# An order of instructions from a list scheduler in the source, in place of the framework's own, for a four-layer hybrid model

## The chip, the cores and the metric

One Trainium2 chip, one core of it. The time is the device time of one execution in microseconds, as a median of several runs; one further execution was taken with the hardware profiler, and all rows of traces come from that one. The core has five engines that each work off their own queue in order: TensorE (PE: matmuls, with PEld for its weight loads), VectorE (DVE), ScalarE (ACT), GpSimd (POOL) and SyncE (SP, which here only issues transfers). They wait for one another by semaphores.

## The reference

A model of two blocks on 256 tokens of width 1024 in float32. Each block has two layers, and each layer is a feed-forward network, a mixer and another feed-forward network, each behind an RMS norm and added to the residual stream. A final norm follows each block.

```python
def swiglu(h, w_gate, w_up, w_down):          # width 1024 -> 2816 -> 1024
    return (jax.nn.silu(h @ w_gate) * (h @ w_up)) @ w_down

def hybrid_layer(x, ...):                     # block 1
    x = x + 0.5 * swiglu(rmsnorm(x, ffn1_norm), ffn1_wg, ffn1_wu, ffn1_wd)
    proj = rmsnorm(x, mix_norm) @ w_in
    na_o = rmsnorm(merge_heads(neighbourhood_attention(...)), na_gain)
    o_fwd = gla_chunked(qg, kg, vg, log_gf, True)
    o_bwd = flip(gla_chunked(flip(qg), flip(kg), flip(vg), flip(log_gb), False))
    gla_o = merge_heads(rmsnorm(o_fwd + o_bwd, gla_gain)) * jax.nn.silu(g_r)
    x = x + jnp.concatenate([na_o, gla_o], axis=-1) @ w_out
    x = x + 0.5 * swiglu(rmsnorm(x, ffn2_norm), ffn2_wg, ffn2_wu, ffn2_wd)
```

Block 2 has the same frame. Its mixer joins a causal forgetting attention, a dilated causal attention with a partial rotary embedding of its queries and keys (the "rope"), and a gated linear recurrence (HGRN2), whose output is multiplied by a sigmoid gate.

## The kernel before

*Activations.* They are kept with features on partitions and the 256 tokens along the free dimension. Every float32 product is made of three products of a faster type: a weight tile `raw` of 128 x 1024 is loaded, ScalarE writes its high part `whi` (L163) and VectorE the remainder `wlo` (L164); the activations are held as `xhl`, high and low side by side. A block of 128 x 128 weights then takes one matmul of 512 columns (high weights by high and low activations) and one of 256 (low weights by high activations). `blocks` issues these two blocks at a time, so four matmuls. `total` (L270, L271) adds the two halves of a finished bank.

*Stages.* There are 12 stages and two final norms, one after another. A feed-forward stage has 44 groups of 8 blocks (gate and up columns in turn; bank tag `acc`, 3 buffers), each followed by ScalarE, VectorE and GpSimd work (`gate`, `up`), and then 176 blocks for the way down (`o`). A mixer stage has 16 such groups and some chunks of projections that come out by rows (`wi`), the attention work and an output projection of 64 blocks (`o`).

*Mixer1* (block 1) runs a gated linear attention in `gla`: `psC`, `psZ` and `log_sigmoid` make the gates (Abs, then Exp and Ln, L650 and L626), `cumulate` scans them into `C` (L660), GpSimd forms differences of `C` for eight levels (`kq`, L928 to L939), ScalarE takes Exp, VectorE multiplies by keys and queries (L946), and TensorE makes the scores `psA`. The first of the `psA` need keys and queries that `columns` writes (L564). Beside it `na` runs the neighbourhood attention: `psS`, a softmax, `psP`, and values whose slabs are moved by transfers on the SP queue (`slabs`). Its keys come from `columns`, too (L560).

*Mixer2* (block 2) runs `hgrn` with the same level scheme (`X`, differences on GpSimd at L1155 to L1160, products at L1168 and L1169), and `attention`, which begins with the rope (VectorE, L1195 to L1197) and the transposes `psT` (L228, from `heads_T`).

*Norms.* `Stage.norm` sums squares on TensorE (`psN`), takes a root on GpSimd (L281) and spreads it over partitions on TensorE (`psR`). The matmuls of a stage don't need it; their results are multiplied by it later (`rb`). `feed_parts` writes the next stage's `xhl` (L328, L329), `feed_squares` its squares, whose sum is built on GpSimd (L342).

*What sets the order.* A driver (`Driver.run`) runs through jobs (weight tiles in order) and tasks (generators), and records instructions in the order in which a clock of its own, which counts TensorE's time alone, lets them go on; the table `WAIT` holds estimated latencies. The framework then schedules each engine, with the recorded order as priority and with a timing model of its own. By hand there is more: `later` puts GpSimd's transfers behind the last product of a feed-forward gate, `issue_after` puts set-up work behind a split, and `exp_ln` and `gate` place the loads of ScalarE's function tables (at L622 and L1065). A split is recorded one job ahead (`AHEAD`); `raw`, `whi` and `wlo` have four buffers each.

## Time and profile before

| | us |
|---|---|
| median of three runs | 2082.66 |
| lowest and highest run | 2081.74, 2084.51 |
| the profiled execution | 2085.31 |
| its span, first to last instruction | 2083.2 |
| TensorE busy in the span | 2032.4 |
| VectorE busy | 1546.6 |
| ScalarE busy | 1159.0 |
| GpSimd busy | 504.1 |

In the rows, L217 is the line of every matmul and L228 that of every transpose, so TensorE's work is told apart by tile names. Ends of matmuls are modelled and weight loads (PEld) run beside them. The granted TensorE clock stands at one of two levels, 1.2 or 2.4 GHz; a mean of 0.95 in a stretch says that a tenth of it was granted the lower one. The stages of the profiled execution begin at about 0, 197.9 (Mixer1), 338, 523.7, 702.6 (Mixer1), 843, 1027.6, 1217.5 (Mixer2), 1368.4, 1553.3, 1738.1 (Mixer2) and 1889.5 us.

### The profile page before, as it was taken

Reading aid. Unit: us, or ns where it says so; the run is one execution under the profiler, and the core shown is the slowest. Engines: PE = TensorE matmul, PEld = TensorE weight load, DVE = VectorE, ACT = ScalarE, POOL = GpSimd, SP = SyncE. Lnnn points to the kernel's source line nnn. Section 1 sums busy time; section 2 is a strip of 40 time slices with the busy share of each in tenths; the row PEclk is TensorE's granted clock in tenths of the full one; section 3 lists DMA queues with packets and bytes.
Section 4 is the critical chain, followed back from the end, with each engine's and each line's share of the span. In section 5 each row is a group of like instructions: output and inputs, shape, how many; then the busy total and the mean of one; then the engine's idle time right before and its main releaser. Section 6 shows DMA issues by size and latency. Waiting matters only on the chain.

```text
span 2083.2 us, 34135 instructions
## 1 busy us (share of the span) xinstructions
PE 2032.4 (98%) x12620; PEld 1781.7 (86%) x12620; DVE 1546.6 (74%) x2433; ACT 1159.0 (56%) x2038; POOL 504.1 (24%) x502
## 2 busy tenths in 40 slices
PE   8999899999999999999999998999999999899997
PEld 7888788888888888888888897888888889788886
DVE  7776878786776687876687679687767766968764
ACT  6554556554555556555465464565546546456553
POOL 3451503441221141222232103022112210302210
PEclk9999899999999989999999999999999999999998
DMA  7665445655555544555565553455555555345552
GB/s 230 193 194 179 127 126 187 196 186 191 187 188 191 158 130 132 192 191 186 170 205 187 189 161 99 126 185 190 191 183 192 186 188 161 93 132 183 192 190 94
DMA packets 104631, 357.37 MB, mean 172 GB/s; under 512 B 13460, under 2 KB 15012, under 8 KB 104464
## 3 DMA queue, kind: packets, MB, share of 16 engines
q1 hardware_dynamic: 101040, 352.20, 52.8%
q0 software_dynamic: 3136, 2.47, 0.6%
q8 instruction: 99, 1.62, 0.3%
q14 instruction: 68, 0.56, 0.1%
q10 hardware_dynamic: 288, 0.52, 0.1%
HBM read 351.98 MB, written 1.51 MB: 170 GB/s over the span
## 4 chain that ended last, share of the span: by engine, by line
PE 87%; DVE 6%; ACT 2%; POOL 2%; issue 1%; DMA 0%; SPq 0%; DVEq 0%; ACTq 0%; POOLq 0%
PE acc L217 53%; PE o L217 26%; PE wi L217 3%; DVE wlo L164 2%; PE psS L217 2%; PE psA L217 1%; PE psO L217 1%; DVE xhl L329 1%; ACT whi L163 1%; DVE x L438 1%; POOL kq L938 1%; DVE rope L1195 1%; PE psN L217 0%; PE psP L228 0%; POOL kq L936 0%
## 5 line engine op out<-in xcount | busy, mean ns | idle before, releaser
L163 ACT ACTIVATE whi<-raw 128x1024 fp32r<-128x1024 f32 (+3 forms) x682 | 706.7, 1038 | 710.8 <-PE acc L217 388.9
L217 PE MATMUL acc<-xhl,whi 128*128 128x512 f32 x3328 | 1061.6, 400 | 6.1 <-DVE xhl L329 5.9
L164 DVE TENSOR_TENSOR wlo<-raw,whi 128x1024 fp32r<-128x1024 f32 (+3 forms) x682 | 824.0, 1209 | 321.8 <-ACT whi L163 319.3
L217 PEld LDWEIGHTS acc<-xhl,wlo 128*128 128x128 f32 x3328 | 629.4, 189 | 147.3
L217 PE MATMUL acc<-xhl,wlo 128*128 128x256 f32 x3328 | 660.9, 279 | 0.0
L217 PEld LDWEIGHTS acc<-xhl,whi 128*128 128x128 f32 x3328 | 513.1, 190 | 13.0 <-DVE xhl L329 7.2
L217 PE MATMUL o<-hT,whi 128*128 128x512 f32 x1408 | 442.4, 395 | 0.3 <-DVE hT L259 0.3
L465 POOL TENSOR_TENSOR s<-s,rb 128x256 f32<-128x256 f32 x176 | 242.4, 1377 | 666.2 <-ACT s L464 661.8
L217 PEld LDWEIGHTS o<-hT,wlo 128*128 128x128 f32 x1408 | 264.5, 188 | 62.5
L217 PE MATMUL o<-hT,wlo 128*128 128x256 f32 x1408 | 276.6, 278 | 0.0
L217 PEld LDWEIGHTS o<-hT,whi 128*128 128x128 f32 x1408 | 214.4, 189 | 0.7 <-DVE hT L259 0.7
L342 POOL TENSOR_TENSOR sqs<-sqs,sq 128x256 f32<-128x256 f32 x88 | 79.0, 901 | 485.6 <-ACT sq L340 485.2
L271 DVE TENSOR_TENSOR t<-acc,b 128x256 f32<-128x256 f32 x416 | 172.6, 416 | 9.0 <-ACT b L270 9.0
L270 ACT ACTIVATE b<-acc 128x256 f32<-128x256 f32 x416 | 151.7, 367 | 12.4 <-PE acc L217 12.3
L217 PE MATMUL wi<-whi,xhl 128*128 128x352 f32 (+2 forms) x448 | 122.5, 344 | 0.0
L475 DVE TENSOR_TENSOR t<-t,s 128x256 f32<-128x256 f32 x176 | 75.9, 431 | 46.3 <-POOL s L465 44.9
L438 DVE SCALAR_TENSOR_TENSOR x<-o,x 128x256 f32<-128x256 f32 x192 | 77.8, 419 | 37.6 <-PE o L217 35.8
L217 PEld LDWEIGHTS wi<-whi,xhl 128*128 128x128 f32 x448 | 83.5, 195 | 0.8 <-ACT proj L536 0.2
L217 PE MATMUL o<-xhl,whi 128*128 128x512 f32 x256 | 80.9, 397 | 1.4 <-DVE xhl L259 1.4
L464 ACT ACTIVATE s<-t 128x256 f32<-128x256 f32 x176 | 70.5, 400 | 19.7 <-DVE t L463 19.6
L463 DVE TENSOR_TENSOR t<-t,rb 128x256 f32<-128x256 f32 x176 | 75.3, 428 | 5.3
L259 DVE TENSOR_TENSOR hT<-t,hT 128x256 fp32r<-128x256 f32 x176 | 78.4, 445 | 0.9 <-ACT hT L258 0.9
(234 smaller groups left out, 1453.3 us busy)
## 6 DMA issues: line engine op xcount, KB each, us to landing
raw<-in_gu_dram SPq DMA_DIRECT2D x350, 512.0 KB, 3.4
raw<-in_wd_dram SPq DMA_DIRECT2D x176, 512.0 KB, 3.4
raw<-in_win_dram SPq DMA_DIRECT2D x64, 512.0 KB, 3.6
raw<-in_wo_dram SPq DMA_DIRECT2D x32, 512.0 KB, 3.6
raw<-in_win_dram SPq DMA_DIRECT2D x24, 384.0 KB, 3.1
raw<-in_win_dram SPq DMA_DIRECT2D x24, 352.0 KB, 3.3
raw<-in_win_dram SPq DMA_DIRECT2D x8, 388.0 KB, 3.1
proj<-proj SPq DMA_DIRECT2D x32, 64.0 KB, 2.0
```

The source lines that it names most:

```text
L163: self.mark = nc.scalar.activation(hi[:, s], r[:, s], AF.Copy).ins
L164: self.mark_v = nc.vector.tensor_tensor(lo[:, s], r[:, s], hi[:, s].bitcast(F32), op=OP.subtract).ins
L217: c.nc.tensor.matmul(out, l, r, start=start, stop=stop)
L259: c.nc.vector.tensor_tensor(lo, src, hi.bitcast(F32), op=OP.subtract)
L270: c.nc.scalar.activation(b, ps[:, T:], AF.Copy)
L271: c.nc.vector.tensor_tensor(t, ps[:, :T], b, op=OP.add)
L342: adder.tensor_tensor(self.sq[:, j], self.sq[:, j], d, op=OP.add)
L438: nc.vector.scalar_tensor_tensor(xs, acc[g][:, h * T:(h + 1) * T], scale, xs, op0=OP.mult, op1=OP.add)
L463: nc.vector.tensor_tensor(t, t, self.rb, op=OP.mult)
L464: nc.scalar.activation(s, t, AF.Silu)
L465: c.pool_mark = nc.gpsimd.tensor_tensor(s, s, self.rb, op=OP.mult).ins
L475: nc.vector.tensor_tensor(t, t, self.s, op=OP.mult)
```

## The change

All engine calls go to a `Program`, which records them instead of issuing them. A recorded instruction is an `Op` with its engine, an occupancy, a latency, and the earlier ones that it depends on, found from the regions of the tiles that it reads and writes. Matmuls recorded without another instruction between them form one `Op`; `cut` ends it, after each two blocks among other places. `order` then goes through simulated time: of all engines' instructions whose dependencies are met and whose tiles have a buffer, it takes the one that can start first, and among those of equal start the one recorded first. Tiles of one tag are opened in recorded order. `issue` sends the instructions out in that order under `manual_schedule`, so that the framework keeps it and adds only the waits.

The durations are formulas. `set_table` records the load of a function table whenever an activation's function needs another table than the last; the load waits for the users of the old table, and the users of the new one for it. The driver's order of recording, the tiles, the buffer counts and the arithmetic stay. `later`, `issue_after` and `exp_ln` go.

```diff
+class Program:
+    HOP = 0.06
+    DRAIN = 0.17
+    TABLES = {"E": "natural_log_exp_and_others", "S": "silu_and_others"}
+    FUNCS = {AF.Exp: "E", AF.Ln: "E", AF.Silu: "S", AF.Sin: "S"}
...
+    def cost(self, engine, name, args, kw, out, n):
+        if name == "dma_start":
+            return (1.0 if engine == "gpsimd" else 0.43), 2.0
+        if engine == "scalar":
+            return 0.08 + 0.000865 * n + (0.1 if "accum_out" in kw else 0.0), 0.095
+        if engine == "vector":
+            if name == "tensor_tensor_scan":
+                return 0.32, 0.085
+            return 0.07 + 0.001045 * n, 0.085
+        if engine == "gpsimd":
+            if kw.get("op") is OP.pow:
+                return 0.75 if n < 3 else 1.0, 0.05
+            return (0.15 if n < 64 else 0.3) if name == "memset" else 0.4 + 0.0039 * min(n, 260), 0.05
+        return 0.0, 0.0
...
+    def set_table(self, t):
+        if t == self.table:
+            return
+        self.cut()
+        op = Op(len(self.ops), "scalar")
+        self.ops.append(op)
+        op.calls.append(("preload_act_table_set", (self.TABLES[t],), {}))
+        op.occ, op.lat = 1.28, 0.0
+        for u in self.users:
+            op.deps[u] = False
+        self.table, self.load, self.users = t, op, []
...
+                if r.dtype == F32R:
+                    occ = max(m / 2400.0 + (0.02 if m > 256 else 0.0085), 0.109)
+                else:
+                    occ = 2 * max(m / 1200.0, cols / 1200.0, 0.025) / (2 if mode == (64, 64) else 1) + 0.005
+            if op.mode is not None and op.mode != mode:
+                occ += 0.09
...
+    def order(self):
...
+            for e in stale:
+                best[e] = None
+                for op in avail[e]:
+                    at = opening(op)
+                    if at is None:
+                        continue
+                    est = max(op.ready, at, free[e])
+                    k = (est, op.n)
+                    if best[e] is None or k < best[e][0]:
+                        best[e] = (k, op)
+            stale = set()
+            e = min((x for x in engines if best[x]), key=lambda x: best[x][0])
+            (start, _), op = best[e]
...
+            extra = 0.1 if e == "tensor" and mode not in (None, op.mode) and op.mode else 0.0
...
+            free[e] = start + op.occ + extra
+            end = free[e] + op.lat
+            if op.calls[0][0] == "dma_start":
+                dst = op.calls[0][1][0]
+                size = free_size(dst) * dst.shape[0] * 4
+                dma = max(dma, start + 0.5) + size / 300e3
+                end = dma + 1.3
...
+    def issue(self):
+        for op in self.order():
+            e = getattr(self.nc, op.engine)
...
         while self.next < N or self.tasks:
+            self.c.nc.cut()
             if self.run_task():
...
         for ps, hi, lo, x, first, last in two:
             mm(c, ps[:, :T], lo, x[:, :T], False, last)
+        c.nc.cut()
...
-    def exp_ln(self, after):
-        if self.table is None:
-            with self.c.tc.issue_after(after.ins):
-                self.table = self.c.nc.scalar.preload_act_table_set("natural_log_exp_and_others").ins
...
-    nc = c.nc = tc.nc
+    nc = c.nc = Program(tc.nc)
...
     dr.run()
+    with tc.manual_schedule():
+        nc.issue()
```

## Rows read from the trace of the kernel before

**Rows 1.** The page, busy us (share of the span) and instructions by engine.
```profile
PE 2032.4 (98%) x12620; PEld 1781.7 (86%) x12620; DVE 1546.6 (74%) x2433; ACT 1159.0 (56%) x2038; POOL 504.1 (24%) x502
```

**Rows 2.** Table by stage: stretch, width, busy us by engine, clock, DMA share, GB/s.
```profile
0.00:22.30 22.30, 16.25 (x65) 13.04 (x66) 12.95 (x21) 14.13 (x28) 6.09 (x16) 0.85 0.68 217
...
197.90:338.00 140.10, 132.81 (x1058) 118.57 (x1057) 108.55 (x176) 82.27 (x153) 40.70 (x45) 0.95 0.46 141
...
523.70:702.60 178.90, 178.90 (x1030) 156.17 (x1031) 130.82 (x198) 98.04 (x168) 36.35 (x29) 1.00 0.58 185
...
1027.60:1217.50 189.90, 187.98 (x1076) 164.13 (x1077) 139.84 (x225) 103.54 (x177) 44.09 (x39) 0.99 0.58 187
...
1738.10:1889.50 151.40, 143.97 (x1019) 127.35 (x1020) 120.04 (x210) 88.10 (x174) 26.08 (x25) 0.97 0.41 126
```

**Rows 3.** Chain that ended last, in order of time: start, us, what.
```profile
527.03 114.26 PE acc L217 x656
641.29 61.31 PE o L217 x352
```

**Rows 4.** Waits, whole span: waiter <- waited for, total us, times, longest.
```profile
ACT whi L163 <- PE acc L217: 388.9, 335, 3.4
...
PE psT L228 <- DVE proj L1197: 14.3, 3, 6.8
...
PE psS L217 <- DVE proj L560: 5.9, 2, 3.1
PE acc L217 <- DVE xhl L329: 5.9, 6, 2.8
...
PE psA L217 <- DVE proj L564: 5.4, 2, 2.7
...
PE psR L217 <- POOL rstd L358: 1.9, 1, 1.9
```

**Rows 5.** Table by stretch, columns as in rows 2: Mixer1, then Mixer2 (last).
```profile
208.00:220.00 12.00, 12.00 (x68) 10.15 (x67) 7.85 (x16) 8.02 (x14) 1.81 (x3) 1.00 0.46 144
220.00:231.00 11.00, 8.27 (x62) 7.58 (x61) 7.61 (x11) 3.79 (x5) 11.00 (x15) 0.71 0.30 97
231.00:252.00 21.00, 17.93 (x181) 15.91 (x180) 20.59 (x25) 13.40 (x21) 17.71 (x15) 0.91 0.52 142
...
1778.00:1788.00 10.00, 3.22 (x18) 2.82 (x17) 10.00 (x9) 5.11 (x11) 9.62 (x9) 0.83 0.12 39
```

**Rows 6.** Tile `rope`, whole span: duration ns least/median/most, first and last start.
```profile
L1195 DVE TENSOR_TENSOR rope<-proj,cs x16: 211/1084/1153, 1255.7 to 1781.4; 128x64 f32<-128x64 f32 x16
```

**Rows 7.** GpSimd by line at 1770 to 1788: busy us, mean ns | idle before.
```profile
L1159 POOL TENSOR_TENSOR X<-C 128x512 f32<-128x512 f32 x5 | 5.3, 1063 | 36.6 <-DVE C L660 36.6
```

**Rows 8.** VectorE in order of time, Mixer2: start, us, what.
```profile
1776.66 0.76 DVE L1195 TENSOR_TENSOR rope<-proj,cs 128x64 f32<-128x64 f32 x5
...
1779.36 3.14 DVE L1195 TENSOR_TENSOR rope<-proj,cs 128x64 f32<-128x64 f32 x3
...
1785.52 1.10 DVE L1197 TENSOR_TENSOR proj<-rope 128x64 f32<-128x64 f32 x1
```

**Rows 9.** VectorE and TensorE in order of time, Mixer1, 222 to 226.
```profile
224.80 0.86 DVE L564 SCALAR_TENSOR_TENSOR proj<-t,rb 128x256 f32<-128x256 f32 x1
...
225.72 0.65 PE L217 MATMUL psA<-proj 64*64 64x64 f32 x7 [2.73 <-DVE proj L564]
```

**Rows 10.** Groups by line and form, GpSimd's slowest level term.
```profile
L938 POOL TENSOR_TENSOR kq<-C 128x256 f32<-128x256 f32 x14 | 17.1, 1219 | 0.0
```

**Rows 11.** Groups by line and form: splits, `xhl`, table loads.
```profile
L163 ACT ACTIVATE whi<-raw 128x1024 fp32r<-128x1024 f32 x622 | 658.6, 1060 | 667.3 <-PE acc L217 372.0 <-PE o L217 197.1 <-issue 73.0
...
L329 DVE SCALAR_TENSOR_TENSOR xhl<-x,gains,xhl 128x256 fp32r<-128x256 f32 x88 | 70.6, 809 | 6.8 <-ACT xhl L328 6.8
...
L622 ACT ACT_TABLE_LOAD x4 | 5.1, 1283 | 0.1
```

More of the change, by code (lines that the diff above doesn't have):

```diff
@@ L94, with __init__, _then, __getitem__ @@
     [(g, f) for g in range(EARLY, 8) for f in range(8)]
+class View:
+    __slots__ = ("tile", "shadow", "chain", "made")
+    def __init__(self, tile, shadow, chain=()):
+        self.tile, self.shadow, self.chain, self.made = tile, shadow, chain, None
+    def _then(self, name, *args, **kw):
+        return View(self.tile, getattr(self.shadow, name)(*args, **kw), self.chain + ((name, args, kw),))
+    def __getitem__(self, k):
+        return self._then("__getitem__", k)
+    def rearrange(self, *args, **kw):
+        return self._then("rearrange", *args, **kw)
+    def unsqueeze(self, i):
+        return self._then("unsqueeze", i)
+    def to_broadcast(self, shape):
+        return self._then("to_broadcast", list(shape))
+    def bitcast(self, dt):
+        return self._then("bitcast", dt)
+    def pattern(self, offset, ap):
+        return View(self.tile, self.tile.shadow, self.chain + (("pattern", (offset, ap), {}),))
+    @property
+    def shape(self):
+        return self.shadow.shape
+    @property
+    def dtype(self):
+        return self.shadow.dtype
+    def real(self):
+        if self.made is None:
+            r = self.tile.real()
+            for name, args, kw in self.chain:
+                if name == "pattern":
+                    r = bass.AP(tensor=r.tensor, offset=r.offset + args[0], ap=args[1])
+                else:
+                    r = getattr(r, name)(*args, **kw)
+            self.made = r
+        return self.made
+    def region(self):
+        t = self.tile
+        ap, off = self.shadow.ap, self.shadow.offset
+        p0, f0 = divmod(off, t.row)
+        if any(c[0] == "pattern" for c in self.chain):
+            return 0, 1 << 30, 0, 1 << 30
+        n = ap[0][1] if ap[0][0] == t.row else 1
+        if t.bank:
+            return p0 // 32 * 32, -(-(p0 + n) // 32) * 32, 0, 1 << 30
+        rest = ap[1:] if ap[0][0] == t.row else ap
+        return p0, p0 + n, f0, f0 + 1 + sum((c - 1) * st for st, c in rest)
@@ new lines, with __init__, real @@
+class LazyTile:
+    def __init__(self, pool, shape, dtype, kw, shadow):
+        self.pool, self.shape, self.dtype, self.kw, self.shadow = pool, shape, dtype, kw, shadow
+        self.row = 1
+        for n in shape[1:]:
+            self.row *= n
+        self.bank = pool.bank
+        self.tag = (pool.name, kw["tag"])
+        self.bufs = kw.get("bufs") or pool.bufs
+        self.marks, self.left, self.made, self.opened, self.index, self.end = [], 0, None, False, None, 0.0
+    def real(self):
+        if self.made is None:
+            self.made = self.pool.pool.tile(list(self.shape), self.dtype, **self.kw)
+        return self.made
@@ new lines, with __init__, tile @@
+class Pool:
+    def __init__(self, program, pool, name, bufs, bank=False):
+        self.program, self.pool, self.name, self.bufs, self.bank = program, pool, name, bufs, bank
+    def tile(self, shape, dtype, **kw):
+        t = LazyTile(self, shape, dtype, kw, self.program.shadow(tuple(shape), dtype))
+        return View(t, t.shadow)
+class Op:
+    __slots__ = ("n", "engine", "calls", "occ", "lat", "deps", "after", "wait", "ready", "start", "tiles", "mode")
+    def __init__(self, n, engine):
+        self.n, self.engine, self.calls, self.occ, self.lat = n, engine, [], 0.0, 0.0
+        self.deps, self.after, self.wait, self.ready, self.start = {}, [], 0, 0.0, None
+        self.tiles, self.mode = {}, None
@@ L864, in prepare @@
         self.wg = c.cp.tile([33, 512], F32, tag="wgate", name="wgate")
-        with c.later():
-            nc.gpsimd.dma_start(self.wg, a["wgate"][l])
+        nc.gpsimd.dma_start(self.wg, a["wgate"][l])
         rp = a["rpb"]
@@ L1097, in hgrn @@
             e = t2(c, "lse")
-            last = nc.scalar.activation(e, z, AF.Abs)
+            nc.scalar.activation(e, z, AF.Abs)
             gs.append(z)
@@ L1290, in setup1 @@
     yield 20.0
-    with c.later():
-        c.mk = c.cp.tile([P, 7, 64], I32, tag="mk", name="mk1")
-        nc.gpsimd.dma_start(c.mk, a["mk1"])
-        c.nam = c.cp.tile([P, 4, 32], F32, tag="nam", name="nam")
-        nc.gpsimd.dma_start(c.nam, a["nam"])
+    c.mk = c.cp.tile([P, 7, 64], I32, tag="mk", name="mk1")
+    nc.gpsimd.dma_start(c.mk, a["mk1"])
+    c.nam = c.cp.tile([P, 4, 32], F32, tag="nam", name="nam")
+    nc.gpsimd.dma_start(c.nam, a["nam"])
     c.dr.fire("set1")
```

308 lines of the change are left out of this document (225 added, 83 removed).

## The prediction

> **What bounds the kernel now.** I read the page's busy times first, then the busy table by stage, then the chain of waits, then the list of what TensorE waited for. TensorE is busy 98% of the span and VectorE 74% [rows 1], so the kernel is TensorE's, and an order of instructions can only give back what TensorE does not use. The table by stage says where that is [rows 2]. In a feed-forward stage there is nothing: 178.90 us wide, 178.90 busy, clock 1.00. The chain agrees: 656 matmuls, all `acc`, stand in one piece of 114.26 us without a wait, 352 of `o` in 61.31 [rows 3], which is 348.3 ns for each pair of a 512-wide and a 256-wide matmul in both. That pitch is the floor of the eight feed-forward stages: (704 + 352) / 2 pairs x 0.3483 = 183.9 us each, 1,471 of 2083 us, and no order changes it.
>
> What is lost is in the rest [rows 2]. A Mixer1 layer has 140.10 - 132.81 = 7.3 us of idle TensorE and a mean clock of 0.95: a tenth of the layer, 14 us, at 1.2 GHz instead of 2.4, which costs at most 7.0 us. Together 14.3, and there are two such layers: 28.6. A Mixer2 layer has 7.4 us idle and a clock of 0.97: 9.1 us at 1.2 GHz, at most 4.5 us; together 11.9, two layers: 23.8. The stage after the first block's final norm loses 1.9 us idle and, at 0.99, up to 1.9 by the clock: 3.8. In the list of TensorE's waits [rows 4] stage starts wait for `xhl` 5.9 us, of which I put the longest (2.8) down to the kernel's start, where the input still lands; 3.1 are left. Sum of what an order could give: 28.6 + 23.8 + 3.8 + 3.1 = 59 us, so no order ends below about 2024. The start (22.30 us wide, 16.25 busy [rows 2]) and the tail are chains of a landing input and of a last normalisation; I leave both as they are, within 1 us.
>
> **What holds TensorE up there.** All large waits name VectorE: `psT` for the rope 14.3 us, `psS` for L560 5.9, `psA` for L564 5.4 [rows 4]. TensorE goes in the order of the recorded program, so it stands at an attention matmul while weights for later groups wait. But in the same stretches VectorE is full: 20.59 of 21.00 us at 231 to 252, and 10.00 of 10.00 us at 1778 to 1788, where TensorE does 3.22 [rows 5]. And it is full of slow work. A rope product of 64 elements takes 211 ns at best and 1084 in the median [rows 6], because GpSimd's subtractions of 1.06 us stand back to back beside it [rows 7]: three products take 3.14 us [rows 8]. The same holds, weaker, for L564 in Mixer1: 0.86 us for one product of 256 columns, where the wait of 2.73 us ended [rows 9].
>
> This is where the Trainium skill speaks against the change: the page "SBUF — State Buffer", section "SBUF: two separate sides", says that a VectorE instruction with two SBUF inputs and a GpSimd instruction exclude each other for a whole instruction, whichever starts first. The trace agrees (211 against 1084 ns). A scheduler that gives each engine its own duration can't see such a lock; by that rule the waits for the rope would stay, and that part of the sum is zero.
>
> **The change part by part.** *TensorE's order.* Its work is cut into units of four matmuls (two pairs, 2 x 0.348 = 0.7 us), and the scheduler starts the first unit that is ready by its own clock, the earliest recorded first. In Mixer1 the groups behind the waiting `psA` and `psS` need only `xhl` and split weights, so filler exists: at 220 to 231 ScalarE is busy 3.79 of 11 us and at 208 to 220 VectorE 7.85 of 12 [rows 5], and splits can be moved there up to the four buffers. In addition the gate chain that starts the level work (`psC`, `psZ`, Abs, Exp, Ln, `C`) no longer waits behind whole groups of 2.8 us. And the level terms on GpSimd are charged at 0.4 + 0.0039 x 256 = 1.40 us by the code, where the trace has 1.22 or less [rows 10]: they are late in the plan and early on the chip, so TensorE isn't led to them too soon. Against it: VectorE full for 21 us cannot be ordered away, and a filler used early is missing at the end of the layer, where the output projection waits for the attention. The two bounds are 0 and 14.3 us per layer. I take half, 7 us, since of the 7.3 idle the first wait (2.73) has an idle VectorE and ScalarE ahead of it and the second (3.1 of the 5.9 [rows 4]) has not. Two layers: 14 us.
>
> In Mixer2 the plan charges a rope product 0.07 + 0.001045 x 64 = 0.14 us. Eight of them and four sums of the same size are 12 x 0.14 = 1.7 us in the plan, and took 10 us on the chip (1776.66 to 1786.6) [rows 8]. So `psT` is put where TensorE reaches it at the same time as now or earlier, and the wait stays. Bounds: the whole 11.9 us per layer, if the rope gets in front of the subtractions, and minus 3 us, if TensorE gets there at about 1777 and not, as now, at 1786.6 - 6.8 = 1779.8 [rows 4, 8]. I take 2 us per layer, for the small waits around it: 4 us.
>
> *Norms and stage starts.* After the final norm TensorE stands at `psR` for a root on GpSimd, 1.9 us [rows 4], while further groups need no root for their matmuls; the sums are taken out of the banks without it. The scheduler can go past it: 3.5 of 3.8 us. At the other stage starts, a third group can be begun while `xhl` is late; but `xhl` on VectorE takes 0.81 us in the mean [rows 11], and the plan has 0.42 for it. I take 2.5 of 3.1.
>
> *Table loads.* They become instructions that wait only for the last user of the old table, so the load of 1.28 us ahead of the first Exp [rows 11] goes into ScalarE's idle time instead of between Abs and Exp. It is on the gate chain and inside the 7 and 2 us above, not added.
>
> *Splits and loads.* In the feed-forward stages ScalarE already waits 388.9 us for a buffer that TensorE frees [rows 4]: splits can't go earlier, and the weight loads on SP, which wait for the raw tiles that the splits free, neither. Zero, hidden by those buffers; if the plan put a split just ahead of a chain step, one split of 1.06 us [rows 11] would be its price, and VectorE's idle quarter covers it. The slab transfers of Mixer1 go in the same SP queue, and one that the plan puts behind a raw load that has no tile yet would hold them up; I take nothing for it. GpSimd's small transfers lose their fixed place behind a feed-forward product; GpSimd waits most of such a stage, so nothing either.
>
> *Finer interleaving.* Changing between narrow and full matmuls is charged 0.09 to 0.1 us in the plan. The trace has no row for it alone; a mixer that changed 20 times more would pay 2 us, and none if units of one kind stay together, as they do when they come ready together. I take zero and keep 4 layers x 2 = 8 us for the range.
>
> Sum: 14 + 4 + 3.5 + 2.5 = 24 us. The profiled execution took 2085.31 us (span 2083.2); it would take about 2061, and the median of the runs, 2082.66, becomes 2058.5.
>
> **The rivals.** *A. Nearly all is filled.* The plan starts Mixer1's chain so early that its VectorE work spreads out, and the rope gets ahead of the subtractions: 45 to 59 of the 59 us come back, 2024 to 2038. For it: the idle VectorE at 208 to 220. Against it: the full VectorE later on.
>
> *B. The waits move.* The order is another, but VectorE's full stretches decide in both mixers, and what is filled early is waited for before the output projection: only the norms and stage starts gain, 4 to 8 us, or nothing: 2075 to 2083. That the order comes out nearly as now, because with ties the recorded order decides, gives the same time.
>
> *C. Slower: the plan's clock is wrong and the order is fixed.* A unit that stands where the plan has it ready waits for all that the chip is late. The 24 rope instructions of the two layers are about 24 x 0.87 = 21 us later than at their best [rows 6], and 14.3 of it is waited for now [rows 4]; if `psT` is put at the planned end, the rest comes on top: 7 us. At 11 stage starts `xhl` is 0.4 us later than planned: 4 us more, if the units behind it are put up to it. Together with the 8 us of changes, if nothing is gained in Mixer1: 2083 + 7 + 4, up to 8 = 2094 to 2102. It decides as soon as the lateness that newly hits TensorE exceeds the idle time filled, some 5 us per mixer.
>
> **How the numbers follow.** The forecast, a partial gain of 13 to 38 us (2045 to 2070), 0.45. A, with what lies between it and the forecast (2024 to 2045): 0.17. B with the rest of the middle (2070 to 2087): 0.17. C: 0.21. The range 2030 to 2094 leaves out the end of A and most of C. A measurement of this kernel tells a change from none at about 0.2%, 4.2 us: faster means below 2078.5 (0.45 + 0.17 + half of B, 0.08 = 0.70), the same 0.09, slower 0.21.
>
> **What would show it.** Right: the 656-matmul pieces stay at 114.26 us; in the table by stage Mixer1 gets near 133 us and Mixer2 stays near 149; the `psT` wait for L1197 is still the largest of TensorE's waits; the `psR` wait is gone. Wrong: `psT` no longer waits (A), a new wait for `xhl` L259 ahead of the output projection of 5 us or more (B), or idle TensorE inside the feed-forward stages, which I hold to be impossible to gain and easy to lose (C).

## The result and the profile after

The kernel after takes 2061.46 us in the median of four runs (2060.64 to 2062.75), the kernel before, on the same chip, 2083.24. The ratio is 0.9896, with a 95% interval from 0.9879 to 0.9913. The forecast was 2058.5, with a range from 2030 to 2094. The profiled execution of after took 2062.75 us with a span of 2061.0, 22.2 less than before's span of 2083.2.

In the trace of after every instruction has the line of the helper that issues it (L448, in other kernels of this study a line near it), so it is read by tile names. The page's busy times, which answer to [rows 1], and the two pieces of the chain that answer to [rows 3]:

```profile
PE 2023.6 (98%) x12620; PEld 1773.1 (86%) x12620; DVE 1581.3 (77%) x2433; ACT 1198.2 (58%) x2039; POOL 486.8 (24%) x502
```

```profile
337.14 114.27 PE acc L448 x656
451.41 61.31 PE o L448 x352
```

The floor stands: the 656 matmuls take 114.27 us, as before. So the 22 us came from other places, and a table by stage shows which. For it both traces are cut at the last matmul of each `o`, so that a stage's start belongs to it. Columns: stretch, width, then busy us of PE, PEld, DVE, ACT and POOL with their instruction counts, PE's granted clock, DMA share, GB/s. First the kernel before, in this order: the kernel's start with the first feed-forward stage, Mixer1 of the first and second layer, the feed-forward stage after the first block's final norm, Mixer2 of the third and fourth layer.

```profile
0.00:197.90 197.90, 191.85 (x1074) 166.27 (x1075) 144.75 (x216) 110.59 (x192) 73.69 (x94) 0.98 0.63 200
197.90:331.30 133.40, 126.77 (x1023) 113.52 (x1023) 103.56 (x169) 79.14 (x147) 39.15 (x43) 0.95 0.45 137
...
702.60:836.20 133.60, 127.22 (x1023) 113.97 (x1023) 103.60 (x169) 79.16 (x147) 39.19 (x45) 0.95 0.44 136
...
1022.00:1211.50 189.50, 187.58 (x1073) 163.74 (x1073) 139.84 (x225) 103.54 (x178) 44.96 (x40) 0.99 0.58 188
1211.50:1361.60 150.10, 142.57 (x1020) 126.68 (x1019) 119.00 (x220) 87.12 (x170) 26.68 (x29) 0.97 0.41 123
...
1732.20:1882.70 150.50, 143.66 (x1019) 127.33 (x1018) 118.08 (x207) 87.26 (x171) 25.46 (x24) 0.97 0.40 123
```

The same six stages of the kernel after, and between them one plain feed-forward stage (512.70 on):

```profile
0.00:199.00 199.00, 192.99 (x1073) 166.44 (x1074) 150.75 (x228) 116.60 (x194) 73.78 (x104) 1.00 0.64 200
199.00:326.90 127.90, 123.75 (x1024) 110.76 (x1023) 105.97 (x170) 78.74 (x148) 63.66 (x78) 0.97 0.49 147
...
512.70:697.50 184.80, 184.80 (x1066) 161.36 (x1065) 137.62 (x202) 106.54 (x172) 33.67 (x30) 1.00 0.57 185
697.50:819.60 122.10, 120.78 (x1024) 108.49 (x1023) 103.55 (x172) 79.60 (x152) 43.34 (x46) 1.00 0.50 155
...
1005.40:1193.20 187.80, 186.51 (x1074) 162.53 (x1073) 142.60 (x215) 106.36 (x172) 38.15 (x33) 1.00 0.58 185
1193.20:1342.00 148.80, 142.95 (x1019) 127.17 (x1018) 119.67 (x218) 87.00 (x171) 28.36 (x28) 0.97 0.40 125
...
1712.50:1860.40 147.90, 143.24 (x1020) 127.42 (x1019) 118.74 (x208) 88.23 (x172) 26.53 (x23) 0.97 0.42 126
```

By widths: Mixer1 gains 5.5 and 11.5 us, Mixer2 1.3 and 2.6, the stage after the final norm 1.7, and the start loses 1.1. That is 21.5 of the 22.2; the six plain feed-forward stages hold the other 0.7, all of it in the one behind the first Mixer1 layer (186.5 before, 185.8 after). In the second Mixer1 layer TensorE's idle time went from 6.4 to 1.3 us and the clock from 0.95 to 1.00, with the same VectorE work (103.6 us). VectorE's full stretch was not shortened: before, it is busy 26.35 of the 30 us from 722.6 on, where TensorE does 25.40; after, it is busy 39.50 of the 40 us from 717.5 on, and TensorE does 38.68. TensorE only does not stand in front of it any more. Mixer2 still has 4.7 to 5.9 us idle and a clock of 0.97.

What TensorE waited for in after (waiter <- waited for, total us, times, longest), to be read against [rows 4]:

```profile
PE psT L448 <- DVE proj L448: 10.0, 4, 4.9
PE acc L448 <- DVE xhl L448: 2.9, 6, 1.6
PE o L448 <- DVE xhl L448: 2.8, 2, 1.8
...
PE psA L448 <- DVE kq L448: 2.6, 4, 0.7
PE acc L448 <- DVE t L448: 1.6, 2, 1.1
...
PE psR L448 <- POOL rstd L448: 0.8, 2, 0.6
```

The waits of `psS` (5.9) and `psA` (5.4) for `proj` are gone, `psT` for the rope is still the largest. Three questions follow: is it the order of TensorE that gained, why is Mixer1's first layer 5.8 us longer than its second, and what holds Mixer2.

### The profile page after: what moved, and what is told of

Its sections match the earlier page's. It is cut to its first block, busy times and chain, and to the rows that moved or that the text cites. A ratio compares the mean times of both kernels' runs of the same rounds, so it can differ in the third digit from the quotient of the medians.

```text
span 2061.0 us, 33817 instructions
## 1 busy us (share of the span) xinstructions
PE 2023.6 (98%) x12620; PEld 1773.1 (86%) x12620; DVE 1581.3 (77%) x2433; ACT 1198.2 (58%) x2039; POOL 486.8 (24%) x502
## 4 chain that ended last, share of the span: by engine, by line
PE 86%; DVE 9%; ACT 2%; issue 2%; DMA 1%; SPq 0%; POOL 0%; DVEq 0%; ACTq 0%
PE acc L448 51%; PE o L448 26%; PE wi L448 3%; DVE wlo L448 3%; PE psS L448 2%; PE psA L448 1%; DVE x L448 1%; DVE xhl L448 1%; PE psO L448 1%; DVE proj L448 1%; ACT whi L448 1%; DVE t L448 1%; PE psP L448 1%; DVE rope L448 0%; DVE C L448 0%
## 5 line engine op out<-in xcount | busy, mean ns | idle before, releaser
L448 PE MATMUL acc<-xhl,whi 128*128 128x512 f32 x3328 | 1059.8, 399 | 5.5 <-DVE xhl L448 2.9
L448 DVE TENSOR_TENSOR wlo<-raw,whi 128x1024 fp32r<-128x1024 f32 (+3 forms) x682 | 829.7, 1218 | 192.8 <-ACT whi L448 181.1
L448 ACT ACTIVATE whi<-raw 128x1024 fp32r<-128x1024 f32 (+3 forms) x682 | 704.7, 1034 | 329.6 <-PE o L448 207.1
L448 PEld LDWEIGHTS acc<-xhl,wlo 128*128 128x128 f32 x3328 | 627.9, 189 | 146.9 <-DVE wlo L448 0.3
L448 PE MATMUL acc<-xhl,wlo 128*128 128x256 f32 x3328 | 660.0, 279 | 0.0
L448 PEld LDWEIGHTS acc<-xhl,whi 128*128 128x128 f32 x3328 | 511.5, 190 | 13.7 <-DVE xhl L448 6.3
L448 PE MATMUL o<-hT,whi 128*128 128x512 f32 x1408 | 442.2, 395 | 0.0
L448 POOL TENSOR_TENSOR s<-s,rb 128x256 f32<-128x256 f32 x176 | 214.9, 1221 | 686.0 <-ACT s L448 686.0
L448 ACT ACTIVATE b<-acc 128x256 f32<-128x256 f32 x416 | 158.1, 382 | 334.6 <-PE acc L448 334.3
L448 PEld LDWEIGHTS o<-hT,wlo 128*128 128x128 f32 x1408 | 264.5, 188 | 62.5
L448 DVE TENSOR_TENSOR t<-acc,b 128x256 f32<-128x256 f32 x416 | 174.6, 422 | 135.0 <-ACT b L448 134.8
L448 PE MATMUL o<-hT,wlo 128*128 128x256 f32 x1408 | 276.6, 278 | 0.0
L448 PEld LDWEIGHTS o<-hT,whi 128*128 128x128 f32 x1408 | 214.3, 189 | 0.0
L448 POOL TENSOR_TENSOR sqs<-sqs,sq 128x256 f32<-128x256 f32 x88 | 77.7, 887 | 506.1 <-ACT sq L448 505.4
L448 PE MATMUL wi<-whi,xhl 128*128 128x352 f32 (+2 forms) x448 | 119.8, 336 | 0.0
L448 DVE SCALAR_TENSOR_TENSOR x<-o,x 128x256 f32<-128x256 f32 x192 | 78.7, 420 | 41.0 <-PE o L448 38.6
L448 DVE TENSOR_TENSOR t<-t,rb 128x256 f32<-128x256 f32 x200 | 87.3, 436 | 6.3
L448 ACT ACTIVATE hT<-t 128x256 fp32r<-128x256 f32 x176 | 73.5, 418 | 26.2 <-DVE t L448 16.1
L448 ACT ACTIVATE s<-t 128x256 f32<-128x256 f32 x176 | 73.8, 419 | 25.8 <-DVE t L448 16.7
L448 DVE TENSOR_TENSOR t<-t,s 128x256 f32<-128x256 f32 x176 | 74.7, 425 | 18.2 <-POOL s L448 1.1
L448 PE MATMUL o<-xhl,whi 128*128 128x512 f32 x256 | 82.8, 405 | 2.8 <-DVE xhl L448 2.8
L448 DVE TENSOR_TENSOR hT<-t,hT 128x256 fp32r<-128x256 f32 x176 | 83.0, 472 | 0.0
```

The costliest lines, as they stand in the source:

```text
L448: getattr(e, name)(*args, **kw)
```

## The experiments

Each edit is made on the kernel after, and each ratio is to the kernel before on the same chip, with its 95% interval. Five of the kernels below keep the set-up work in its old place; they say so. The runs are spread over several chips, on which the median of before lies between 2081.95 and 2083.41 us, and an interval is about 3 us to either side. So two medians within 3 us of each other are not told apart, and there I go by the widths of stages; those of the plain feed-forward stages agree within 0.1 us in all runs but the one with flat durations.

**TensorE in recorded order.** All else is scheduled as in after, but TensorE takes its units as they were recorded.

```diff
+        queue = [op for op in ops if op.engine == "tensor"][::-1]
...
                 for op in avail[e]:
+                    if e == "tensor" and op is not queue[-1]:
+                        continue
```

> TensorE's units stay in the recorded order; the other engines keep the list order. Theory 1 (the prediction's): the gain in Mixer1 comes from TensorE going past a unit that is not ready. Then it falls away: the Mixer1 layers go back towards 140 us and the median to 2072 or more. Theory 2: the changed kernel's own plan has only 53 of 2762 TensorE units behind one recorded later, so the gain comes from the order on VectorE and ScalarE. Then Mixer1 stays within 3 us of the changed kernel, only the stage after the final norm gives back its 2 us, and the median is 2062 to 2066.

Measured: 2081.42 us, ratio 0.9990 [0.9980, 0.9999], 20 us over after. The start, the two Mixer1 layers and the two Mixer2 layers, then the largest wait of the `psA`:

```profile
0.00:204.40 204.40, 195.01 (x1073) 168.28 (x1074) 149.87 (x228) 116.74 (x194) 75.14 (x104) 0.97 0.62 195
204.40:337.40 133.00, 125.14 (x1024) 111.80 (x1023) 104.33 (x170) 78.40 (x148) 58.61 (x79) 0.97 0.46 141
...
708.00:838.00 130.00, 123.16 (x1023) 109.99 (x1022) 103.27 (x172) 78.89 (x152) 38.82 (x46) 0.99 0.47 145
...
1212.10:1360.00 147.90, 143.41 (x1019) 127.49 (x1018) 118.10 (x218) 87.18 (x171) 28.29 (x29) 0.97 0.42 126
...
1730.60:1878.80 148.20, 143.68 (x1019) 127.61 (x1018) 116.19 (x208) 88.02 (x172) 27.23 (x24) 0.97 0.43 126
```

```profile
PE psA L453 <- DVE kq L453: 6.9, 6, 3.0
```

Mixer1 gives back 5.1 and 7.9 of its 17.0, and TensorE stands in front of `kq` again (2.6 us in after, 6.9 here). The start loses another 5.4, but there the change had gained nothing: its 204.4 us are 6.5 more than before, so in the start this fixed order costs time of its own, and the 20 us are not all gain taken back. Mixer2 stays as it is in after: its gain of 4 us comes from the order on the other engines, not from TensorE's going past a waiting unit.

**The table load behind the Abs.** Only the load's new freedom is undone: it waits again for the last ScalarE instruction recorded before it.

```diff
+        last = [o for o in self.ops[:-1] if o.engine == "scalar"][-1:]
+        if t == "E":
+            for o in last:
+                op.deps[o] = False
```

> The table load for Exp and Ln waits for the last recorded ScalarE instruction, the Abs, as in the kernel before; nothing else changes in the recording. If the load on the gate chain is a large part of the gain (theory 2, with the chain as its mechanism), Mixer1 gets longer by 1.3 to 4 us a layer and the median is 2064 to 2070. If the chain has slack there (theory 1), 2060 to 2063.

Measured: 2064.34 us, 0.9910 [0.9896, 0.9925], 2.9 over after by the medians and 1.6 by the spans (2062.6), no more than the noise. Mixer1's first layer is 127.6 us wide instead of 127.9, its second 123.1 instead of 122.1. The median lies at the lower end of what theory 2 expected, the layers do not reach its 1.3 us. The load's place is at most a small part of Mixer1's gain.

**The set-up work back in its place.** The two fixed places that the change took away are put into the plan as dependencies: GpSimd's set-up transfers and the bias sums behind the last product of a gate, the angle work behind a split.

```diff
+    @contextmanager
+    def issue_after(self, mark):
+        self.behind.append(mark)
+        yield
+        self.behind.pop()
...
+        for m in self.behind:
+            if m is not None and m is not op and m.engine == engine:
+                op.deps[m] = False
...
-                nc.gpsimd.dma_start(b0[p0:p0 + 16, h // 2], src)
+                with c.later():
+                    nc.gpsimd.dma_start(b0[p0:p0 + 16, h // 2], src)
```

> The set-up work (GpSimd's transfers and bias sums behind a feed-forward product, the other set-up behind a split) gets its former ordering edges back, now as edges in the plan. Theory: the first Mixer1 layer, 5.9 us longer than the second, loses that to the next layer's bias sums, which the scheduler moved beside the hi/lo chain at its end. Then the first layer comes down to the second's length, the wait of 0.76 us in the first feed-forward stage goes, and the median is 2053 to 2057. Rival: the layers differ for another reason; 2060 to 2063.

Measured: 2054.71 us, 0.9859 [0.9844, 0.9873], 6.8 under after. The three kinds of set-up work were moved together, not one by one. The start and the two Mixer1 layers:

```profile
0.00:197.80 197.80, 191.58 (x1073) 165.33 (x1074) 147.60 (x216) 116.82 (x194) 69.50 (x94) 0.99 0.63 200
197.80:319.90 122.10, 120.78 (x1024) 108.47 (x1023) 102.74 (x170) 78.39 (x147) 41.75 (x42) 1.00 0.48 151
...
690.60:812.70 122.10, 120.80 (x1023) 108.50 (x1022) 102.90 (x170) 78.47 (x147) 42.24 (x45) 1.00 0.48 149
```

Both layers are now 122.1 wide. The start is 1.2 us shorter, but that is not shown to be the edit's: with the set-up work in its place it is 197.8 us here and 196.2 to 199.5 in the four runs below, against 199.0 in after. Shown is only that TensorE loses 0.5 us between 80 and 120 us in after and nothing here. What had happened in after is in its trace, in order of time (start, us, engine, instruction, in brackets the idle time before it): at the end of the first Mixer1 layer the scheduler had put the next layer's four bias sums, since their engine was free.

```profile
295.79 5.64 POOL L448 TENSOR_TENSOR bias<-b,nam 128x512 f32<-128x512 f32 x4 [1.33 <-DMA b<-skew]
...
298.54 1.75 DVE L448 TENSOR_TENSOR xhl<-S,xhl 128x512 fp32r<-128x512 f32 x1
...
300.44 0.70 PE L448 MATMUL o<-xhl,whi 128*128 128x512 f32 x2 [1.83 <-DVE xhl L448]
...
796.03 0.68 DVE L448 TENSOR_TENSOR xhl<-S,xhl 128x512 fp32r<-128x512 f32 x1
...
796.95 0.63 PE L448 MATMUL o<-xhl,whi 128*128 128x512 f32 x2
```

Beside them one `xhl` took 1.75 us; in the second layer, without them, it took 0.68, and the output projection began without a wait. After that wait the clock was granted at the lower level for 6.8 us, and in the second layer never (1.00 in its row above):

```profile
301.50:308.30 6.80, 5.93 (x18) 5.06 (x19) 5.95 (x12) 3.69 (x7) 0.00 (x0) 0.50 0.21 49
```

**The plan told of the rope.** Rope products and sums are charged 1.0 us each, not 0.14.

```diff
+            if name == "tensor_tensor" and n == 64:
+                return 1.0, 0.085
```

> The plan charges a rope product on VectorE 0.14 us, from its fit, where the trace of after shows up to 1.2 us. Here the plan charges the sixteen rope products and eight rope sums and differences (the products and sums of 64 elements) 1.0 us each, and nothing else is changed; the planned TensorE is 11 us longer, since at the rope the plan has nothing left to fill with. Theory 1 (the wait at the rope in Mixer2 comes of the plan's ignorance of the lock, and told of it the scheduler keeps back other work for it): the wait of psT for proj, 10.0 us in after, falls under 3 us and the time to 2049 to 2055 us. Theory 2 (VectorE's queue is full there, so that what is put ahead of the rope waits instead, and nothing is left to keep back): the waits stay at 8 to 15 us, on psT or on another tile, and the time is 2058 to 2070 us.

Measured: 2055.31 us, 0.9864 [0.9848, 0.9880]. The Mixer2 layers are 145.9 and 144.7 us wide, 2.9 and 3.2 less than in after, and

```profile
PE psT L450 <- DVE proj L450: 4.9, 4, 2.1
```

The wait was halved, not removed: between the two theories, the time just above the first's range. The single products still take up to 1.16 us; the plan only no longer puts `psT` into that time.

**Fewer rope instructions.** The two halves of the tokens in one instruction of 128 elements.

```diff
-            cb = c.cs[:, 0, i].unsqueeze(1).to_broadcast([P, 8, 8])
+        cb, sb = [c.cs[:, j].unsqueeze(2).to_broadcast([P, 2, 8, 8]) for j in range(2)]
```

> The rope of both token halves is done in one go: 6 instructions of 128 elements in place of 12 of 64. Theory: each of these waits for one GpSimd instruction, so the time goes by their number; the rope takes 5 us less in each Mixer2 layer, TensorE's wait at psT falls from 10.0 us in two layers to 3 or less, and the median is 2049 to 2055. Rival: VectorE is full of splits there anyway, and TensorE waits for those instead; 2058 to 2062.

Measured: 2059.36 us, 0.9882 [0.9867, 0.9897]; `psT` still waits 8.8 us. Duration in ns, least, median, most:

```profile
L448 DVE TENSOR_TENSOR rope<-proj,cs x8: 1150/1182/1195, 1238.4 to 1760.0; 128x128 f32<-128x128 f32 x8
```

An instruction of double size takes what one of 64 took before at the median (1084 [rows 6]), so a product pays about one GpSimd instruction, with 128 elements as with 64. Half as many hardly shortened the wait, and not the layers (148.1 and 148.4 us, 148.8 and 147.9 in after); I take it that the splits and products of VectorE in the same queue pay instead, as the rival said, but this run does not show it by itself.

**One SBUF input.** The rope's products and sums are replaced by instructions that read one operand; the kernel leaves out the rotation.

```diff
-                nc.vector.tensor_tensor(dst, x, y, op=OP.mult)
+                nc.vector.tensor_scalar(dst, x, 0.5, None, op0=OP.mult)
```

> The rope's twelve instructions read one SBUF operand in place of two (each only scales its input by a constant; the rotation by cosine and sine is left out). Theory: VectorE and GpSimd exclude each other because of the second SBUF operand; then the rope instructions take 0.25 us or less beside GpSimd's subtractions, TensorE's wait at psT falls from 10.0 to 3 us or less and the median is 2050 to 2055. Rival 1: any instruction of VectorE that reads SBUF is held up; nothing changes, 2059 to 2062. Rival 2: the splits before and after the rope are held up in the same way and set the wait; the rope gets short and the median is 2057 to 2060.

Measured: 2061.66 us, 0.9900 [0.9885, 0.9915], no change to after; `psT` waits 9.5 us.

```profile
L448 DVE TENSOR_SCALAR rope<-proj x16: 180/182/1157, 1238.7 to 1763.4; 128x64 f32<-128x64 f32 x16
L448 DVE TENSOR_SCALAR proj<-rope x8: 180/966/1612, 1241.0 to 1764.3; 128x64 f32<-128x64 f32 x8
```

The instructions with one input were held up as well, up to 1.61 us: 11 of the 24 take over 0.4 us, as many as with two inputs in after. The second operand alone is not the cause.

**The rope ahead of the subtractions.** Set-up work in its place as above, and GpSimd's first `X` of a Mixer2 layer waits for the rope's result.

```diff
+            if m == self.LEVELS[0]:
+                y = self.turned_half[:, 7, 7:8]
+                sub(X[:, 0, 0:1], y, y, op=OP.add)
...
+        c.dr.fire((self.n, "rope"))
         yield WAIT["rope"]
```

> As the run with the set-up work back in its place, and in Mixer2 GpSimd's first subtraction waits for the rope: one small GpSimd instruction ahead of it reads the rope's last result. Theory: GpSimd's back-to-back subtractions are what keeps VectorE from splits and rope; without them beside it the rope takes 2.5 us, TensorE's wait at psT falls to 2 us or less in two layers, and each Mixer2 layer loses 4 to 6 us: 2043 to 2047. Rival: the subtractions start 5 to 7 us later and TensorE waits for the levels' psA in place of psT; 2053 to 2057.

Measured: 2057.32 us, 0.9876 [0.9860, 0.9892]. The rope is at its best, and `psT` is out of the list of waits, with a new one at its head. The two Mixer2 layers behind it:

```profile
L458 DVE TENSOR_TENSOR rope<-proj,cs x16: 211/218/226, 1229.9 to 1753.4; 128x64 f32<-128x64 f32 x16
```

```profile
PE psA L458 <- DVE X L458: 10.3, 3, 4.9
```

```profile
1188.10:1339.40 151.30, 144.66 (x1019) 129.12 (x1019) 119.47 (x221) 87.90 (x171) 30.56 (x30) 0.95 0.40 123
...
1709.90:1855.10 145.20, 139.72 (x1020) 125.32 (x1019) 118.50 (x208) 88.51 (x172) 28.92 (x25) 0.99 0.43 128
```

Against the run with the set-up work alone (147.9 and 148.0) one layer lost 3.4 us and the other gained 2.8. The lateness moved from `psT` to `psA`: the subtractions are later, and beside them VectorE's work is held up in the rope's place (a product of `X` and `proj` takes 0.68 us at the least and up to 1.61).

**The subtractions on VectorE.** So the contest itself was taken away. Set-up work in its place, and

```diff
-            sub = nc.gpsimd.tensor_tensor
+            sub = nc.vector.tensor_tensor
```

for `X`, in Mixer2 alone. With the set-up work alone, the two Mixer2 layers and `X` were

```profile
1186.50:1334.40 147.90, 143.04 (x1019) 127.16 (x1018) 118.29 (x221) 87.24 (x171) 27.87 (x28) 0.97 0.41 126
...
1705.00:1853.00 148.00, 143.29 (x1020) 127.48 (x1019) 118.89 (x208) 88.29 (x172) 26.55 (x24) 0.97 0.41 126
```

```profile
L458 POOL TENSOR_TENSOR X<-C x30: 1044/1114/2174, 1225.4 to 1772.6; 128x512 f32<-128x512 f32 x30
```

> The set-up work held back as in the run of that alone (2054.7 us), and Mixer2's thirty subtractions that make X, 128 by 512 each, on VectorE instead of GpSimd, where they take 1.34 us on the mean, planned at the fit's VectorE price of 0.6 us. So no GpSimd subtraction stands beside the rope and the splits of Mixer2 any more, and VectorE gets about 30 x 0.6 = 18 us more of its own work in the two layers, 9 each. Theory 1 (what costs Mixer2 its last 3 to 5 us a layer is the lock between the two engines): rope products back near 0.2 us, splits near 1.2 us, the wait of psT for proj gone, each Mixer2 layer 143 to 146 us against 148.0, and the time 2046 to 2051 us. Theory 2 (VectorE's own queue is the limit there, in whichever way it is filled): the layers stay at 147 to 151 us and the time at 2053 to 2060 us, with the wait on psT or on psA for X.

Measured: 2038.53 us, 0.9786 [0.9771, 0.9800], 16.2 us under the run with the set-up work alone, and the fastest kernel of this study. It went beyond what the first theory expected. Rope and `X` by duration, the wait, and the two Mixer2 layers:

```profile
L458 DVE TENSOR_TENSOR rope<-proj,cs x16: 207/215/222, 1227.9 to 1741.2; 128x64 f32<-128x64 f32 x16
...
L458 DVE TENSOR_TENSOR X<-C x30: 669/680/682, 1224.7 to 1763.7; 128x512 f32<-128x512 f32 x30
```

```profile
PE psT L458 <- DVE proj L458: 0.5, 1, 0.5
```

```profile
1184.80:1325.00 140.20, 139.36 (x1019) 124.39 (x1018) 116.81 (x236) 87.45 (x171) 8.73 (x14) 1.00 0.45 133
...
1695.50:1836.10 140.60, 139.35 (x1020) 124.41 (x1019) 115.96 (x223) 88.11 (x172) 6.85 (x9) 1.00 0.44 132
```

Each layer became 7.4 to 7.7 us shorter (the start another 1.6, which the edit does not touch), TensorE's idle time fell to about 1, and the clock stays at 1.00. VectorE has 15 instructions of 0.68 us more in a layer, 10.2 us, and yet is busy 116.81 us instead of 118.29 in the run with the set-up work alone. So in that layer the contest had cost VectorE about 10.2 + 118.29 - 116.81 = 11.7 us, and by the same sum 13.1 in the other. TensorE had not waited for `X` in the run with the set-up work alone, so it is not that `X` itself comes sooner. About 7.5 us of a Mixer2 layer were this contest; the best of the orders tried here, with the rope charged, had given back 2.9 and 3.2.

**The same in Mixer1.** On top of that, `kq` goes to VectorE by the same edit in `gla`.

> The same in Mixer1: on top of the run with X on VectorE (2038.5 us), the sixty subtractions that make kq, 128 by 256 each, go from GpSimd, where they take 1.16 us at the median, to VectorE, where the fit prices them at 0.34 us: 20 us more VectorE work, 10 a layer, planned TensorE 4 us longer. There TensorE waits 2.6 us in all for kq in the run before, and each layer is at 122.1 us. Theory 1 (any GpSimd subtraction beside VectorE's splits and products costs VectorE more than doing it itself): the waits of psA for kq go, each Mixer1 layer falls to 119 to 121 us, and the time to 2034 to 2037 us. Theory 2 (the lock costs only where TensorE waits for VectorE's next result, as at the rope, and Mixer1 has filler enough): layers at 121.5 to 125 us and the time at 2038 to 2045 us, with 2 us or more of waits on kq or on another tile of VectorE's.

Measured: 2041.41 us, 0.9808 [0.9792, 0.9825], 2.9 over the run without it by the medians and 1.6 by the spans. The two Mixer1 layers, to be set against 122.1 each:

```profile
196.40:318.80 122.40, 121.52 (x1024) 108.76 (x1023) 105.77 (x200) 77.99 (x147) 8.47 (x12) 1.00 0.49 150
...
689.50:812.50 123.00, 121.71 (x1024) 108.86 (x1023) 105.72 (x200) 78.00 (x147) 8.93 (x14) 1.00 0.48 149
```

The second theory holds: the layers are 0.3 and 0.9 us longer, not shorter. VectorE had paid here too (30 subtractions of 0.415 us, the median in this run, are 12.5 us more work, and busy rose by 3.0 us), but TensorE had other work to do in that time, and had waited for `kq` only 2.6 us in all. Of that wait 0.9 is left; what the layers lost is in TensorE's busy time (120.8 to 121.5 and 121.7), and its cause stays open.

**Flat durations.** Every VectorE and ScalarE instruction is planned at 0.5 us and every GpSimd one at 1.0.

```diff
-            return 0.08 + 0.000865 * n + (0.1 if "accum_out" in kw else 0.0), 0.095
...
-            return 0.07 + 0.001045 * n, 0.085
+        if engine in ("scalar", "vector"):
+            return 0.5, 0.09
+        if engine == "gpsimd":
+            return 1.0, 0.05
```

> All durations of VectorE and ScalarE in the plan are 0.5 us and of GpSimd 1.0 us; TensorE's and the transfers' stay. Theory: the fitted durations matter, since a unit that TensorE passes over or takes is chosen by them; the mixers lose most of the gain and the median is 2070 or more. Rival: the list with the recorded order as priority does it, whatever the durations; 2060 to 2066.

Measured: 2184.33 us, 1.0491 [1.0475, 1.0506], 123 us over after. One feed-forward stage, which in after has 184.80 us and no idle time, and the two waits that are new:

```profile
540.70:741.50 200.80, 193.27 (x1067) 164.40 (x1066) 132.51 (x202) 101.67 (x172) 25.27 (x30) 0.99 0.54 171
```

```profile
PE acc L442 <- DVE t L442: 39.8, 167, 0.8
PE o L442 <- DVE hT L442: 16.9, 8, 2.1
```

Planned with these durations in place of the fitted ones, the kernel loses more than five times what the change gained, but above all in the stages that have nothing to win: eight feed-forward stages lose 13 to 16 us each. The two Mixer1 layers are 128.1 us wide, the first as in after, the second 6 longer, and the two Mixer2 layers are even shorter (146.8 and 147.1). I take the split, planned at 0.5 us where it takes 1.06 [rows 11], to be what puts the emptying of the banks late 167 times; it was not tried by itself.

**Longer units.** TensorE's unit is cut after each call of `blocks` instead of after each two blocks.

```diff
             mm(c, ps[:, :T], lo, x[:, :T], False, last)
-        c.nc.cut()
+    c.nc.cut()
```

> TensorE's unit becomes a whole call of blocks (a group of up to 16 matmuls, 2.8 us) and no longer four matmuls (0.7 us). Theory: going past a waiting unit needs small units, because what is passed in is then late by up to 2.8 us; Mixer1 loses half of what the order of TensorE gave, 3 to 4 us a layer, and the start some of its gain: 2067 to 2073. Rival: the size hardly matters; 2060 to 2064.

Measured: 2058.74 us, 0.9887 [0.9871, 0.9904], 2.7 under after, no more than the noise, and below both expectations. By the widths the Mixer1 layers are at 125.2 and 121.1 (127.9 and 122.1 in after), the stage after the final norm at 187.2 (187.8). The fine units were not what Mixer1 needed; they cost a little.

**Set-up work and longer units together.**

> Two edits put together that were each run alone: the set-up work held back behind the place it had before the change (the run alone gave 2054.7 us, 6 under the change's 2061), and TensorE's unit cut once for a group of blocks instead of once for each (alone 2058.7, 2.7 under). If what they save lies in different places, the start of the span and Mixer1's layer a for the one and Mixer1's layer b and the stage behind the final norm for the other, their sum holds: 2051 to 2053 us. If both take from the same 5.8 us by which Mixer1's layer a is longer than its layer b, the time is that of the first alone: 2054 to 2056 us.

The two edits above in one kernel. Measured: 2051.93 us, 0.9849 [0.9834, 0.9863]. The sum of the times holds, and both Mixer1 layers are at 121.1. Not all of it lies where it was expected: the start is 1.0 us longer than with the set-up work alone, and the Mixer2 layers, at 146.2 and 147.0, are 1.7 and 1.0 shorter.

## Why the prediction was right, and where not

*Mixer1, 14 us.* The mechanism was right: 13.0 of the 17.0 us gained go when TensorE keeps the recorded order, and the table load, by the widths, is worth 0.7 in the two layers together. The term was mis-sized in both directions. I took half of what a layer had lost because I held that VectorE's 21 full us [rows 5] could not be ordered away. They were not, but nothing of TensorE had to stand in them: the second layer got back 11.5 us, most of its 6.4 us idle (5.1) and all of its clock (6.4 us less of busy time). In size that is what rival A described, for one stage; its reason, a VectorE whose work spreads out, is not seen.

*"GpSimd waits most of such a stage, so nothing either".* This step failed, and it hid part of the first error. It looked at the transfers alone and at GpSimd alone. Behind them come the bias sums, and what they delay is VectorE: 5.8 us in the first Mixer1 layer, given back by the run that puts the set-up work in its place. Start and tail were taken as 0 within 1 us; the start with the first feed-forward stage came out at minus 1.1. There 0.5 us of TensorE's waiting is this set-up work, and the rest is within what the start varies from run to run.

*Mixer2, 4 us.* 3.9 came, and the reason for so little was right: `psT` is still the largest wait, and the lock between the engines holds Mixer2. The path of the 4 us was another than I thought, since TensorE's recorded order keeps them. Two readings were too large. The 10 us that I gave the rope in one layer [rows 8] hold a split of 2.13 us and, in its first line, five products in 0.76. The lateness of the 24 rope instructions in rival C takes the median for all, but only 16 of them were held up; all 24 took 19.2 us, so it is about 19.2 - 24 x 0.21 = 14 us, not 21. Neither is in the sum. Of the rule from the Trainium skill (page "SBUF — State Buffer", section "SBUF: two separate sides"), that one of the two engines has the shared port for a whole instruction: the trace agrees, with 1084 ns for a rope product at the median beside the subtractions [rows 6] and 215 when they are gone. The bounds that I gave for `psT` (all 11.9 us a layer, if the rope gets ahead) were attached to the wrong place: ahead of the subtractions the rope was free, and the layers were still 151.3 and 145.2 us wide. VectorE's whole queue was held, not the rope. The Trainium skill (page "Perfetto Trace Analysis", section "Optimizing Scalar/DVE Operations") says that moving work between VectorE and GpSimd might not help, because they share a read port. The traces go further: the subtractions of `X` on GpSimd cost the two Mixer2 layers 15.1 us against the same work on VectorE.

*Final norm, 3.5 us.* 1.7 came. The wait of `psR` there went from 1.9 to 0.2 (0.6 of the 0.8 in after is at the kernel's start), but in its place TensorE waits 1.1 us at once for a `t` that empties a bank: what is pushed past the norm must be taken out of the banks by VectorE, and that was not in the sum.

*Stage starts, 2.5 us.* 0.7 came. Of the 5.9 us in before, 3.4 lie at the kernel's start, not 2.8, and 0.6 to 0.7 at each of four stages behind a mixer; in after it is 1.9 at the start and 0.9 at the four together. So the waits fell as the term said, but the width did so in one of the four stages only (186.5 to 185.8); the others have 185.8, 185.7 and 185.7 before and 185.8, 185.7 and 185.8 after. Why, stays open. The longer wait of `o` for `xhl` (1.4 us before, 2.8 after) belongs to the bias sums: all of it lies in the first Mixer1 layer, and it is gone with the set-up work in its place.

*Splits and loads, 0.* Right: 184.80 us in both. That an order has nothing to win here and can lose much was shown by the flat durations.

*Finer interleaving, 0.* By the widths the fine units cost 3.7 us in Mixer1 (2.0 with the set-up work in its place) and 0.6 after the final norm, within the 8 that I kept for the range. Whether that is the change between narrow and full matmuls, no run shows.

The errors nearly cancel: Mixer1 would have given 9 us more than forecast, had its first layer gained like its second (23 instead of 14); against that stand 6.0 lost in the first layer, 1.1 at the start, 1.8 at the norm, 1.8 at the starts and 0.1 in Mixer2, together 10.8, so 22.2 instead of 24. That the total came so near is in part luck: of the four terms only Mixer2's came as forecast, and by another path. Rival C's mechanism, a plan that is too early for the rope, is real: charging the rope won 6 us. But the wait had been longer in before's order (14.3 us against 10.0), so the time did not go that way.

## What to carry to other kernels

An order gains where an engine stands behind a waiting instruction while it has other work that is ready; it gains little where two engines hold each other, because the plan gives each its own duration: 3.9 us in Mixer2, and 6 more when the plan was told. Before ordering around such a contest, price taking it away: thirty subtractions moved to the busier engine gave 15.1 us in the layers where they stand, against 21.8 for the whole scheduler, and moving sixty more, for which TensorE had waited only 2.6 us, made their layers 1.2 us longer. And when hand-made places fall away, follow the work behind them to the engine that it slows, not only to the one that it runs on.

## What the runs showed of the hardware

- Beside GpSimd's subtractions in a row, a small VectorE product of two operands in SBUF takes about one GpSimd instruction (1.1 us): 1084 ns at the median for 64 elements [rows 6], 1182 for 128, against 215 for 64 with the subtractions gone. Instructions with one SBUF input are held up as well: 180 ns at the least, 1612 at the most, 11 of 24 over 400 ns, as with two inputs in after.
- The contest costs VectorE more than the moved work: 15 subtractions of 1.1 us on GpSimd had cost it 11.7 and 13.1 us in the two Mixer2 layers, and take 10.2 us on VectorE itself.
- Small set-up work falls into it, too: an angle instruction of 16 elements took 1.26 us beside the bias sums in after's first stage, and 0.18 in before.
- The lower clock went with the waits: as they went away, the granted clock of Mixer1's second layer rose from 0.95 to 1.00, and that of the Mixer2 layers, with `X` on VectorE, from 0.97 to 1.00, worth 3.7 us of TensorE's busy time in a Mixer2 layer (143.04 to 139.36).
